# Heads of 64 columns: products that stream 128 columns and keep 64, in a kernel of three transformer blocks

## The chip, the cores and the metric

One core of a Trainium2 chip. The metric is the device time of one execution of the whole kernel, in microseconds; the time of a kernel is the median over its runs.

## What is computed

Three blocks over a sequence of 512 tokens of width 1024, in float32. Block 1 mixes with forgetting attention (4 heads), RWKV-7 (8 heads) and MoBA attention (4 heads); block 2 with gated linear attention and sparse attention chosen by an indexer (DSA, 8 heads on shared keys and values), then a gated unit and feed-forward parts; block 3 with a bidirectional state-space scan (32 heads in 8 groups) beside a convolution. Every head is 64 wide. What matters here, cut from the reference:

```python
# attention of blocks 1 and 2 (per head, d = 64)
probs = softmax(logits); y = einsum('bhqk,bhkd->bhqd', probs, v)
# RWKV-7, per head and token
removed = einsum('bhvk,bhk->bhv', state, kk_t)
state = state * w_t - removed (kk_t * a_t)^T + v_t k_t^T
y_t = einsum('bhvk,bhk->bhv', state, r_t)
y = ((y - mean) * rsqrt(var + GN_EPS)) * ln_w + ln_b      # over the 64 of a head
# scan, one direction, chunks of 128
mix = scores[..., None] * decay * dt
y_diag = einsum('bclsgr,bcsgrp->bclgrp', mix, xs)          # p = 64
y_off = einsum('bclgn,bcgrpn->bclgrp', cm, h_prev) * exp(la)
```

## The kernel before, in words

Activations lie as feature x token tiles of 128 x 512 or token x feature tiles of 128 x 512, four blocks of 128 tokens side by side. Two heads of 64 make a pair of 128, so a tile of tokens holds a pair's two heads side by side in each block of 128 columns. A projection weight is loaded by SP, split by ScalarE and VectorE into a high and a low part, and each of its products is three matmuls (L296 to L298, L370 to L372). The products named below are plain fp32.

- **Attention** (`attn`, L550 to L606; block 1 twice through `causal_attn`, block 2 through DSA). For each pair, query block and head: logits, softmax, transposes of the probabilities, and the product with the values (L583), which sums over the key blocks into `[:, :64]` of a PSUM tile; the evacuation scales the 64 columns into `yt` (L588 in block 1). The step before the value product is emitted one head ahead.
- **RWKV** (`rwkv_chain`, L803 to L906), one chain for each of four pairs, chunks of 128 tokens: decayed keys against values (`pv`, L841, copied by ScalarE, L842), the chain over chunks with `pU` (L855, read negated by ScalarE, L856) and the state, then the output `pY`: for each chunk the state's product (L877, both heads in 128 columns) and for each head the two products of the chunk itself (L879, L880; 64 columns each). Mean and variance over each head's 64 columns follow on VectorE, with ScalarE's square and POOL's power between (L885 to L894), then transposes (L898), the affine step, the bonus rows loaded by SP (L901), and the gate (L905). Each chain has two PSUM buffers under its tag.
- **Scan** (`ssm_group`, L1451 to L1534), 8 groups of 4 heads by 4 chunks: decays by ScalarE, added by POOL, multiplied with the scores by VectorE into `E` (L1504), four products with 64 columns each (`pY`, L1507), the state's product (`pO`, L1510), and VectorE's sums (L1518 and after). L1531 transposes the result.
- **Modulation sums** (`mod_tile`, L383 load, L384 row sum on VectorE) are spread over the stages; in block 1 they stand beside the RWKV tail.

What sets the order: strings of letters (`ORDER`, `REST`, `ORDER2`, `ORDER3`) say which generator emits its next step, and a scheduler then orders the instructions of all engines with its own costs for each; so a product of other shape moves its neighbours too. Each engine works its own queue in order; SP's queue holds the loads.

Of the kernel before, what the change touches and what calls it, by code (L numbers as in the profile page):

```python
# [12 lines left out]
OP = mybir.AluOpType  # L13
# [182 lines left out]
class Kern:  # L196
# [357 lines left out]
    def attn(self, npr, logits, value, ys, put, tag2="pt"):  # L554
# [16 lines left out]
        def second(pr, qt, hh, P, rinv):  # L571
# [9 lines left out]
            o = self.pst(tag2)[:, :64]  # L581
            for kb in range(qt + 1):
                nc.tensor.matmul(o, PT[:, kb * 128:(kb + 1) * 128], value(pr, hh, kb), start=kb == 0, stop=kb == qt)  # L583
# [26 lines left out]
    def causal_attn(self, q, k, v, ys, FHL=None):  # L610
# [16 lines left out]
        return self.attn(2, logits, lambda pr, hh, kb: v[kb][:, (2 * pr + hh) * 64:(2 * pr + hh) * 64 + 64], ys, put)  # L627
# [174 lines left out]
    def rwkv_chain(self, i, K, gl, out, tag):  # L802
# [35 lines left out]
        pv = ps()  # L838
        for hh in range(2):
            for m in range(4):  # L840
                nc.tensor.matmul(pv[:, hs(m, hh)], Ak[hh][:, MS[m]], tok["v"][:, hs(m, hh)], start=True, stop=True)  # L841
        nc.scalar.copy(RV, pv)  # L842
# [4 lines left out]
        nU = vM  # L847
        for n, ms in enumerate(MS):
# [5 lines left out]
            for hh in range(2):  # L854
                nc.tensor.matmul(pU[:, 64 * hh:64 * hh + 64], TF[hh][:, ms], RV[:, hs(n, hh)], start=True, stop=True)  # L855
            nc.scalar.mul(nU[:, ms], pU[:, 0:128], -1.0)  # L856
# [17 lines left out]
        pY = ps()  # L874
        for m, ms in enumerate(MS):
            if m:
                nc.tensor.matmul(pY[:, ms], RO[:, ms], S[:, ms], start=True, stop=False)  # L877
            for hh in range(2):
                nc.tensor.matmul(pY[:, hs(m, hh)], A[hh][0][:, ms], tok["v"][:, hs(m, hh)], start=m == 0, stop=False)  # L879
                nc.tensor.matmul(pY[:, hs(m, hh)], A[hh][1][:, ms], nU[:, hs(m, hh)], start=False, stop=m == 0 or hh == 1)  # L880
# [4 lines left out]
        nc.vector.tensor_reduce(sm, mh(pY), AX.X, OP.add)  # L885
        nc.vector.tensor_scalar(sm, sm, 1.0 / 64, None, OP.mult)
        b8 = lambda t: t.rearrange("p (a o) -> p a o", o=1).to_broadcast([128, 8, 64])
        nc.vector.tensor_tensor(y8, mh(pY), b8(sm), OP.subtract)
# [563 lines left out]
    def ssm_group(self, g, xs, dtv, pre=()):  # L1452
# [38 lines left out]
        for c in range(4):  # L1491
# [14 lines left out]
            for r in range(4):  # L1506
                nc.tensor.matmul(pY[:, r * 64:(r + 1) * 64], M[:, r * 128:(r + 1) * 128], XT[c][:, r * 64:(r + 1) * 64], start=True, stop=True)  # L1507
# [10 lines left out]
            nc.vector.tensor_tensor(y, pY[:, :256], sk, OP.add)  # L1518
# [258 lines left out]
    def dsa(self, bq, bk2, bv, masks, ys):  # L1777
# [9 lines left out]
        return self.attn(4, logits, lambda pr, hh, kb: bv[:, kb], ys, lambda p: self.split(p, "scalar", "vector", tag="g"), "pb")  # L1787
# [127 lines left out]
    def block2_attn(self):  # L1915
# [21 lines left out]
        bv = self.small([128, 4, 64], "bv", bufs=1)  # L1937
# [6 lines left out]
        nc.scalar.copy(bv, pt[:, :, 0:64])  # L1944
# [186 lines left out]
```

## Time and profile before

| what | value |
|---|---|
| median of 3 runs | 3138.52 us (3137.82 to 3141.42) |
| the profiled execution | 3126.9 us |
| its span | 3125.1 us |
| mean granted clock of TensorE | 0.977 |
| TensorE busy | 2941.1 us (94%) |
| VectorE busy | 2044.3 us (65%) |
| ScalarE busy | 1158.7 us (37%) |
| GpSimd busy | 663.6 us (21%) |

Busy time is a union over an engine's instructions; the profile's two shares of TensorE (PE for matmuls, PEld for weight loads) overlap. Lines are those of the kernel before. The granted clock is the share of full speed that TensorE was given in a stretch. A fp32 matmul leaves two records and two weight loads.

### The profile page before, as it was taken

The numbers are of one execution on the slowest core, as the hardware profiler recorded it, in microseconds if no ns is written. First come the engines' busy times: TensorE is split into PE (matmuls) and PEld (weight loads), VectorE is DVE, ScalarE is ACT, GpSimd is POOL, SyncE is SP. The second block draws the span as 40 slices with busy tenths as digits, with TensorE's granted clock in tenths as the row PEclk, the third lists the DMA queues.
The fourth block names the chain that finished last, engine by engine and source line by source line (L and its number), as shares of the span: only waits on it lengthen the run. The fifth ranks groups of instructions, "written<-read, shape, count | busy, mean of one in ns | idle before, by whom it ended". The sixth has DMA issues, their size and how long they took to land. (4 is left out here: it accounts for less than half of the span.)

```text
span 3125.1 us, 39947 instructions
## 1 busy us (share of the span) xinstructions
PE 2941.1 (94%) x15254; PEld 2428.6 (78%) x15254; DVE 2044.3 (65%) x3398; ACT 1158.7 (37%) x1927; POOL 663.6 (21%) x574
## 2 busy tenths in 40 slices
PE   5999999999989979999999999999899999989998
PEld 3778778888867778888889788887777777777877
DVE  7766477666467677566655565464888989886254
ACT  4433433323333544332334243233433333434232
POOL 3222011000234253200011110002223343441011
PEclk9998999999999999999999999999999999999999
DMA  6334034363312133236343222332222122212342
GB/s 223 102 106 144 11 112 157 110 207 95 99 58 88 44 99 98 88 93 204 100 152 101 88 82 90 106 91 79 85 71 66 63 78 71 71 58 88 115 128 81
DMA packets 137376, 312.53 MB, mean 100 GB/s; under 512 B 25504, under 2 KB 51680, under 8 KB 137184
## 3 DMA queue, kind: packets, MB, share of 16 engines
q1 hardware_dynamic: 137184, 309.98, 32.0%
q8 instruction: 120, 1.97, 0.3%
q14 instruction: 72, 0.59, 0.1%
HBM read 296.82 MB, written 13.11 MB: 99 GB/s over the span
## 5 line engine op out<-in xcount | busy, mean ns | idle before, releaser
L275 ACT CAST wh<-wr 128x1024 fp32r<-128x1024 f32 (+2 forms) x457 | 455.6, 997 | 1010.7 <-PE mm L297 517.8
L277 DVE TENSOR_TENSOR wl<-wr,wh 128x1024 fp32r<-128x1024 f32 (+2 forms) x415 | 499.3, 1203 | 503.6 <-ACT wh L275 496.0
L298 PE MATMUL mm<-hi,wl 128*128 128x512 f32 (+1 forms) x1780 | 683.4, 384 | 10.4 <-DVE wl L277 10.3
L296 PE MATMUL mm<-hi,wh 128*128 128x512 f32 (+1 forms) x1780 | 685.7, 386 | 4.5 <-DVE cv L1217 2.6
L297 PE MATMUL mm<-lo,wh 128*128 128x512 f32 (+1 forms) x1780 | 684.3, 385 | 1.3 <-POOL lo L494 0.6
L298 PEld LDWEIGHTS mm<-hi,wl 128*128 128x128 f32 x1780 | 339.3, 191 | 77.9 <-DVE wl L277 12.8
L296 PEld LDWEIGHTS mm<-hi,wh 128*128 128x128 f32 x1780 | 339.0, 191 | 74.5 <-issue 3.7
L297 PEld LDWEIGHTS mm<-lo,wh 128*128 128x128 f32 x1780 | 339.5, 191 | 68.7 <-issue 2.2
L286 POOL CAST hi<-us 128x512 fp32r<-128x512 f32 x66 | 42.4, 643 | 872.8 <-DVE us L1194 855.1
L298 PE MATMUL pt<-hi,wl 128*128 128x512 f32 (+1 forms) x517 | 188.5, 365 | 4.0 <-DVE wl L277 4.0
L296 PE MATMUL pt<-hi,wh 128*128 128x512 f32 (+1 forms) x517 | 188.1, 364 | 0.0
L297 PE MATMUL pt<-lo,wh 128*128 128x512 f32 (+1 forms) x517 | 187.6, 363 | 0.0
L296 PE MATMUL pb<-hi,wh 128*128 128x512 f32 (+1 forms) x477 | 178.2, 374 | 0.0
L297 PE MATMUL pb<-lo,wh 128*128 128x512 f32 (+1 forms) x477 | 177.9, 373 | 0.0
L298 PE MATMUL pb<-hi,wl 128*128 128x512 f32 (+1 forms) x477 | 177.8, 373 | 0.0
L1415 DVE SCALAR_TENSOR_TENSOR u<-csg,vec,u 128x400 f32<-128x400 f32 (+7 forms) x208 | 165.2, 796 | 2.5
L298 PE MATMUL pa<-hi,wl 128*128 128x512 f32 (+1 forms) x420 | 160.9, 383 | 0.0
L296 PE MATMUL pa<-hi,wh 128*128 128x512 f32 (+1 forms) x420 | 160.6, 382 | 0.0
L297 PE MATMUL pa<-lo,wh 128*128 128x512 f32 (+1 forms) x420 | 160.6, 382 | 0.0
L370 PE MATMUL mm<-wh,hi 128*128 128x256 f32 (+1 forms) x512 | 150.6, 295 | 9.4 <-DVE sar L1984 3.0
L371 PE MATMUL mm<-wl,hi 128*128 128x256 f32 (+1 forms) x512 | 147.7, 289 | 0.5 <-DVE wl L277 0.5
L372 PE MATMUL mm<-wh,lo 128*128 128x256 f32 (+1 forms) x512 | 147.7, 289 | 0.3 <-DVE lo L494 0.3
(758 smaller groups left out, 5589.7 us busy)
## 6 DMA issues: line engine op xcount, KB each, us to landing
wr<-f_up SPq DMA_DIRECT2D x88, 512.0 KB, 3.5
wm<-w_mod SPq DMA_DIRECT2D x152, 256.0 KB, 5.1
wr<-w3x SPq DMA_DIRECT2D x56, 512.0 KB, 3.5
wr<-w_up SPq DMA_DIRECT2D x44, 512.0 KB, 3.6
wr<-w3c SPq DMA_DIRECT2D x40, 512.0 KB, 3.6
wr<-f_down SPq DMA_DIRECT2D x32, 512.0 KB, 3.5
wr<-w SPq DMA_DIRECT2D x29, 512.0 KB, 3.7
wr<-w_down SPq DMA_DIRECT2D x16, 512.0 KB, 3.6
```

The source lines that it names most:

```text
L275: nc.scalar.copy(h, r)
L277: self.lo_engs[self.nlo % len(self.lo_engs)].tensor_tensor(l, r, h.bitcast(FT), OP.subtract)
L286: getattr(nc, hi_eng).tensor_copy(h, x)
L296: nc.tensor.matmul(ps, a, xh, start=first and i == 0, stop=False)
L297: nc.tensor.matmul(ps, a, xl, start=False, stop=False)
L298: nc.tensor.matmul(ps, b, xh, start=False, stop=last and i == n - 1)
L370: nc.tensor.matmul(ps, xh, a, start=k == 0, stop=False)
L371: nc.tensor.matmul(ps, xh, b, start=False, stop=False)
L372: nc.tensor.matmul(ps, xl, a, start=False, stop=k == K - 1)
L1415: nc.vector.scalar_tensor_tensor(r8(o)[:, :, a:b], src, w(k), r8(o)[:, :, a:b], OP.mult, OP.add)
```

## The change

Each product with 64 moving columns streams both heads of a pair (in DSA, with its shared values, the next key block too, with a fifth block of zeros at the end) into twice the PSUM columns, and the reader of the product takes the 64 columns that count. In RWKV `pv` and `pY` become one PSUM tile for each head; the state's product is then made for both of them, and the reads of `pY` are split into two ops each.

```diff
--- before.py
+++ after.py
@@ -578,9 +578,12 @@
                 nc.scalar.copy(PT, psP)
             else:
                 nc.vector.tensor_copy(PT, psP)
-            o = self.pst(tag2)[:, :64]
+
+            o = self.pst(tag2)[:, :128]
             for kb in range(qt + 1):
-                nc.tensor.matmul(o, PT[:, kb * 128:(kb + 1) * 128], value(pr, hh, kb), start=kb == 0, stop=kb == qt)
+                v, at = value(pr, hh, kb)
+                nc.tensor.matmul(o, PT[:, kb * 128:(kb + 1) * 128], v, start=kb == 0, stop=kb == qt)
+            o = o[:, at:at + 64]
             if pr not in yts:
                 yts[pr] = self.small([128, 512], "yt", bufs=1)
             yo = yts[pr][:, qt * 128 + hh * 64:qt * 128 + hh * 64 + 64]
@@ -624,7 +627,7 @@
                 nc.tensor.matmul(ps, self.selR[:, h * 128:(h + 1) * 128], FHL[:, :nk], start=False, stop=False)
             nc.tensor.matmul(ps[:, qt * 128:nk], self.identR, self.mnegR, start=False, stop=True)
 
-        return self.attn(2, logits, lambda pr, hh, kb: v[kb][:, (2 * pr + hh) * 64:(2 * pr + hh) * 64 + 64], ys, put)
+        return self.attn(2, logits, lambda pr, hh, kb: (v[kb][:, pr * 128:pr * 128 + 128], 64 * hh), ys, put)
 
 
     def mix_evac(self, ps, j, out):
@@ -835,11 +838,13 @@
 
         RV = self.t2(nm="RV", tag="i")
         Ak = inner(kt, KA, 1)
-        pv = ps()
+
+        of = lambda t, hh: t.rearrange("p (m h d) -> p m h d", m=4, h=2)[:, :, hh]
         for hh in range(2):
-            for m in range(4):
-                nc.tensor.matmul(pv[:, hs(m, hh)], Ak[hh][:, MS[m]], tok["v"][:, hs(m, hh)], start=True, stop=True)
-        nc.scalar.copy(RV, pv)
+            pv = ps()
+            for ms in MS:
+                nc.tensor.matmul(pv[:, ms], Ak[hh][:, ms], tok["v"][:, ms], start=True, stop=True)
+            nc.scalar.copy(of(RV, hh), of(pv, hh))
         yield
 
         S = self.t2(nm="S", tag="h")
@@ -852,8 +857,8 @@
                 nc.vector.tensor_tensor(RV[:, ms], pK[:, 0:128], RV[:, ms], OP.add)
             pU = ps()
             for hh in range(2):
-                nc.tensor.matmul(pU[:, 64 * hh:64 * hh + 64], TF[hh][:, ms], RV[:, hs(n, hh)], start=True, stop=True)
-            nc.scalar.mul(nU[:, ms], pU[:, 0:128], -1.0)
+                nc.tensor.matmul(pU[:, 128 * hh:128 * hh + 128], TF[hh][:, ms], RV[:, ms], start=True, stop=True)
+            nc.scalar.mul(nU[:, ms].rearrange("p (h d) -> p h d", h=2), pU[:, 0:256].rearrange("p (b d) -> p b d", b=4)[:, 0:4:3], -1.0)
             if n < 3:
                 pS = ps()
                 nc.tensor.matmul(pS[:, 0:128], tok["k"][:, ms], tok["v"][:, ms], start=True, stop=False)
@@ -871,21 +876,24 @@
             yield
         A = list(zip(inner(kt, RO, 0), inner(bt, RO, 0, d2, "g")))
         yield
-        pY = ps()
+        pYs = [ps(), ps()]
         for m, ms in enumerate(MS):
-            if m:
-                nc.tensor.matmul(pY[:, ms], RO[:, ms], S[:, ms], start=True, stop=False)
-            for hh in range(2):
-                nc.tensor.matmul(pY[:, hs(m, hh)], A[hh][0][:, ms], tok["v"][:, hs(m, hh)], start=m == 0, stop=False)
-                nc.tensor.matmul(pY[:, hs(m, hh)], A[hh][1][:, ms], nU[:, hs(m, hh)], start=False, stop=m == 0 or hh == 1)
+            for hh, pY in enumerate(pYs):
+                if m:
+                    nc.tensor.matmul(pY[:, ms], RO[:, ms], S[:, ms], start=True, stop=False)
+                nc.tensor.matmul(pY[:, ms], A[hh][0][:, ms], tok["v"][:, ms], start=m == 0, stop=False)
+                nc.tensor.matmul(pY[:, ms], A[hh][1][:, ms], nU[:, ms], start=False, stop=True)
         yt = self.t2(nm="yt")
 
         sm = self.small([128, 8], "gns")
         y8 = mh(yt)
-        nc.vector.tensor_reduce(sm, mh(pY), AX.X, OP.add)
+        sh = sm.rearrange("p (m h) -> p m h", h=2)
+        for hh, pY in enumerate(pYs):
+            nc.vector.tensor_reduce(sh[:, :, hh], of(pY, hh), AX.X, OP.add)
         nc.vector.tensor_scalar(sm, sm, 1.0 / 64, None, OP.mult)
         b8 = lambda t: t.rearrange("p (a o) -> p a o", o=1).to_broadcast([128, 8, 64])
-        nc.vector.tensor_tensor(y8, mh(pY), b8(sm), OP.subtract)
+        for hh, pY in enumerate(pYs):
+            nc.vector.tensor_tensor(of(yt, hh), of(pY, hh), sh[:, :, hh:hh + 1].to_broadcast([128, 4, 64]), OP.subtract)
         nc.scalar.activation(out, yt, AF.Square)
         va = self.small([128, 8], "gnv")
         nc.vector.tensor_reduce(va, out.rearrange("p (a d) -> p a d", d=64), AX.X, OP.add)
@@ -1504,7 +1512,8 @@
             nc.vector.tensor_tensor(v4(M), v4(E[0]), b4(SC[:, cs]), OP.mult)
             pY = self.pst("pt")
             for r in range(4):
-                nc.tensor.matmul(pY[:, r * 64:(r + 1) * 64], M[:, r * 128:(r + 1) * 128], XT[c][:, r * 64:(r + 1) * 64], start=True, stop=True)
+                nc.tensor.matmul(pY[:, r * 128:(r + 1) * 128], M[:, r * 128:(r + 1) * 128], XT[c][:, r // 2 * 128:r // 2 * 128 + 128], start=True, stop=True)
+            pY = pY.rearrange("p (a b q) -> p a b q", a=2, b=4)[:, :, 0:4:3]
             pO = self.pst("pt")
             for d, k in ((0, c), (1, 3 - c)):
                 nc.tensor.matmul(pO[:, d * 256:(d + 1) * 256], Cf[:, cs], H[k][:, d * 256:(d + 1) * 256], start=True, stop=True)
@@ -1515,7 +1524,8 @@
             sk = self.t2(nm="sk", tag="t")[:, :256]
             nc.gpsimd.tensor_tensor(q4(sk), q4(XT[c]), self.dsk[:, 4 * g:4 * g + 4].rearrange("p (h o) -> p h o", o=1).to_broadcast([128, 4, 64]), OP.mult)
             nc.gpsimd.tensor_tensor(T[:, :256], T[:, :256], T[:, 256:], OP.add)
-            nc.vector.tensor_tensor(y, pY[:, :256], sk, OP.add)
+            h4 = lambda t: t.rearrange("p (a b q) -> p a b q", a=2, b=2)
+            nc.vector.tensor_tensor(h4(y), pY, h4(sk), OP.add)
             nc.vector.tensor_tensor(y, y, T[:, :256], OP.add)
             nc.vector.scalar_tensor_tensor(y, y, 0.5, SZ[c // 2][:, (c % 2) * 256:(c % 2 + 1) * 256], OP.mult, OP.mult)
             nc.scalar.activation(sk, y, AF.Square, accum_out=ss[:, c:c + 1])
@@ -1784,7 +1794,7 @@
             nc.tensor.matmul(ps, q[:, qt * 128:nk], bk2[1][:, :nk], start=False, stop=False)
             nc.tensor.matmul(ps, self.identR, self.mnegR if qt == 0 else masks[qt], start=False, stop=True)
 
-        return self.attn(4, logits, lambda pr, hh, kb: bv[:, kb], ys, lambda p: self.split(p, "scalar", "vector", tag="g"), "pb")
+        return self.attn(4, logits, lambda pr, hh, kb: (bv[:, kb:kb + 2], 0), ys, lambda p: self.split(p, "scalar", "vector", tag="g"), "pb")
 
     def gla_decay(self, alr):
 
@@ -1934,14 +1944,15 @@
             nc.scalar.copy(bk2[0][e:e + 64], kk[64:128])
         for e in (0, 64):
             nc.vector.tensor_tensor(bk2[1][e:e + 64], kk[64:128], bk2[0][64:128].bitcast(FT), OP.subtract)
-        bv = self.small([128, 4, 64], "bv", bufs=1)
+        bv = self.small([128, 5, 64], "bv", bufs=1)
+        nc.gpsimd.memset(bv[:, 4], 0.0)
         iw = self.small([128, 4, 4], "iw", bufs=1)
         alr = self.t2(nm="alr")
         nc.gpsimd.memset(alr[0:64], 0.0)
         nc.gpsimd.memset(alr[32:33], 1.0)
         t, pt = self.fm_tok(A["w2s"], 100, xs)
         nc.scalar.copy(alr[0:16], t[64:80])
-        nc.scalar.copy(bv, pt[:, :, 0:64])
+        nc.scalar.copy(bv[:, 0:4], pt[:, :, 0:64])
         nc.scalar.mul(iw, pt[:, :, 96:100], 0.5 * 0.125)
         masks = {}
         idx = self.indexer(iq, ik2, iw, masks)
```

The built order of each engine changes in the three stages that hold these lines. Three places:

TensorE, the output products of RWKV's first chain (`pa` is the chain's PSUM tile, `tokv` the values, `x` the tile that holds U, `S` the state, `RO` the decayed receptance, `pt` attention's), as before:

```order
L879 MATMUL pa_3654<-tokv_2817,Ak_3556 128x64
L880 MATMUL pa_3654<-x_70,Ak_3570 128x64
L879 MATMUL pa_3654<-tokv_2817,Ak_3558 128x64
L880 MATMUL pa_3654<-x_70,Ak_3575 128x64
L877 MATMUL pa_3654<-S_3115,RO_456 128x128
L879 MATMUL pa_3654<-tokv_2817,Ak_3556 128x64
L880 MATMUL pa_3654<-x_70,Ak_3570 128x64
L879 MATMUL pa_3654<-tokv_2817,Ak_3558 128x64
L880 MATMUL pa_3654<-x_70,Ak_3575 128x64
L877 MATMUL pa_3654<-S_3115,RO_456 128x128
```

and now (L883 is before's L877, L884 and L885 are L879 and L880, L696 a product of another chain's blocks):

```order
L884 MATMUL pa_3662<-tokv_2817,Ak_3564 128x128
L885 MATMUL pa_3662<-x_70,Ak_3578 128x128
L883 MATMUL pa_3662<-S_3123,RO_456 128x128
L884 MATMUL pa_3663<-tokv_2817,Ak_3566 128x128
L885 MATMUL pa_3663<-x_70,Ak_3583 128x128
L884 MATMUL pa_3662<-tokv_2817,Ak_3564 128x128
L696 MATMUL mm_3602<-RO_1216,bt_1235 128x128 x3
L696 MATMUL mm_3603<-RO_1216,bt_1235 128x128 x3
L696 MATMUL mm_3602<-RO_1216,bt_1235 128x128
L696 MATMUL mm_3603<-RO_1216,bt_1235 128x128
L885 MATMUL pa_3662<-x_70,Ak_3578 128x128
```

Two PSUM tiles are filled side by side, all with 128 columns; products of other chains stand between.

VectorE, the tail of RWKV, from chain 2's first reduce (`mm_3716`) to chain 3's subtraction, as before (`wm` is a row of the modulation weights, L384; `gns` and `gnv` are sum and variance):

```order
L885 TENSOR_REDUCE gns_3737<-mm_3716 128x8
L384 SCALAR_TENSOR_TENSOR wm_4014,rawo<-wm_4014,act 128x512
L891 TENSOR_REDUCE gnv_3711<-x_75 128x8
L886 TENSOR_SCALAR gns_3737<-gns_3737 128x8
L885 TENSOR_REDUCE gns_3768<-mm_3747 128x8
L892 TENSOR_SCALAR gnv_3711<-gnv_3711 128x8
L888 TENSOR_TENSOR yt_3736<-mm_3716,gns_3737 128x512
L894 TENSOR_TENSOR yt_3705<-yt_3705,gnv_3711 128x512
L886 TENSOR_SCALAR gns_3768<-gns_3768 128x8
L563 TENSOR_REDUCE nmx_3781<-pt_3778 128x1
L891 TENSOR_REDUCE gnv_3742<-x_76 128x8
L888 TENSOR_TENSOR yt_3767<-mm_3747,gns_3768 128x512
```

and now, from chain 2's variance to chain 3's first reduce (`mm_3773`; L892, L899, L900 and L902 are before's L885, L891, L892 and L894):

```order
L384 SCALAR_TENSOR_TENSOR wm_4104,rawo<-wm_4104,act 128x512
L568 RECIPROCAL rinv_3818<-sm_3816 128x1
L384 SCALAR_TENSOR_TENSOR wm_4108,modr<-wm_4108,act 128x512
L899 TENSOR_REDUCE gnv_3768<-x_76 128x8
L1152 TENSOR_TENSOR modr<-modr,rawo 128x1
L384 SCALAR_TENSOR_TENSOR wm_4111,rawo<-wm_4111,act 128x512
L900 TENSOR_SCALAR gnv_3768<-gnv_3768 128x8
L384 SCALAR_TENSOR_TENSOR wm_4152,modr<-wm_4152,act 128x512
L902 TENSOR_TENSOR yt_3760<-yt_3760,gnv_3768 128x512
L1152 TENSOR_TENSOR modr<-modr,rawo 128x1
L384 SCALAR_TENSOR_TENSOR wm_4155,rawo<-wm_4155,act 128x512
L892 TENSOR_REDUCE gns_3798<-mm_3773 128x4
```

Between chain 0's first reduce and chain 3's variance stand 17 rows of L384 now, 6 before, and chain 2's normalisation is finished ahead of chain 3's first reduce.

TensorE, the scan, second group, second chunk (`mm` is the projection beside it, `hi` and `lo` its activations, `wh` and `wl` its weights; `E` the masked decays), as before:

```order
L298 MATMUL mm_19786<-hi_18155,wl_19789 128x512
L296 MATMUL mm_19786<-hi_18157,wh_19788 128x512
L297 MATMUL mm_19786<-lo_18158,wh_19788 128x512
L298 MATMUL mm_19786<-hi_18157,wl_19789 128x512
L1507 MATMUL pt_19768<-tok_19463,E_19764 128x64 x4
L1510 MATMUL pt_19773<-H_19499,sfm_19276 128x256
L1510 MATMUL pt_19773<-H_19505,sfm_19276 128x256
L296 MATMUL mm_19786<-hi_18159,wh_19788 128x512
```

and now (numbers of these tiles are 33 higher; L1515 is before's L1507, L1519 is L1510):

```order
L297 MATMUL mm_19819<-lo_18187,wh_19821 128x512
L298 MATMUL mm_19819<-hi_18186,wl_19822 128x512
L296 MATMUL mm_19819<-hi_18188,wh_19821 128x512
L1515 MATMUL pt_19801<-tok_19496,E_19797 128x128 x4
L1519 MATMUL pt_19806<-H_19532,sfm_19309 128x256
L1519 MATMUL pt_19806<-H_19538,sfm_19309 128x256
L297 MATMUL mm_19819<-lo_18189,wh_19821 128x512
L298 MATMUL mm_19819<-hi_18188,wl_19822 128x512
```

Before, the four products follow the last matmul with `hi_18157`; now they follow the first with the tile that was `hi_18155` (18188 - 33): five matmuls earlier.

## Rows read from the trace of the kernel before

**Rows 1.** The page, part 1: busy time, share of the span and instructions of TensorE.

```profile
PE 2941.1 (94%) x15254; PEld 2428.6 (78%) x15254; DVE 2044.3 (65%) x3398; ACT 1158.7 (37%) x1927; POOL 663.6 (21%) x574
```

**Rows 2.** Windows: stretch, busy of PE, PEld, DVE, ACT, POOL, granted clock, DMA.

```profile
313.00:437.00 124.00, 121.61 (x890) 97.61 (x889) 62.09 (x181) 48.31 (x143) 9.87 (x12) 1.00 0.15 50
405.00:428.00 23.00, 23.00 (x212) 21.65 (x210) 16.50 (x50) 4.19 (x12) 2.01 (x1) 1.00 0.41 137
437.00:450.00 13.00, 8.93 (x37) 6.91 (x38) 8.73 (x17) 4.67 (x10) 6.01 (x5) 0.74 0.07 21
450.00:480.00 30.00, 30.00 (x132) 24.16 (x131) 25.41 (x57) 11.83 (x17) 5.94 (x4) 1.00 0.51 158
1090.00:1250.00 160.00, 135.97 (x928) 123.13 (x927) 119.53 (x215) 71.89 (x142) 67.09 (x42) 0.95 0.32 99
2270.00:2840.00 570.00, 531.54 (x2709) 428.13 (x2708) 501.43 (x704) 214.25 (x371) 212.20 (x194) 0.97 0.22 70
```

**Rows 3.** Timeline of TensorE, 420.5 to 422.2 us: start, length, line, operands, records merged.

```profile
420.66 0.44 PE L877 MATMUL mm<-S,RO 128*128 128x128 f32 x2
...
421.55 0.39 PE L880 MATMUL mm<-x,Ak 128*128 128x64 f32 x2
421.77 0.44 PE L877 MATMUL mm<-S,RO 128*128 128x128 f32 x2
```

**Rows 4.** Timeline of TensorE at 2373 and 2482 us: eight records each.

```profile
2372.97 1.10 PE L1507 MATMUL pt<-tok,E 128*128 128x64 f32 x8
2481.90 1.06 PE L1472 MATMUL pa<-sfm,sfm 128*128 128x128 f32 x8
```

**Rows 5.** Chain of waits, 2268 to 2278 us: start, length, what.

```profile
2273.03 0.84 PE pt L1507 x8
2273.87 0.92 PE pt L1510 x4
```

**Rows 6.** Lines L1507 and L1472: durations in ns, least, median, most.

```profile
L1507 PEld LDWEIGHTS pt<-tok,E x256: 186/192/338, 2272.8 to 2821.7; 128*128 128x128 f32 x128
L1507 PE MATMUL pt<-tok,E x256: 218/275/422, 2272.9 to 2821.7; 128*128 128x64 f32 x128
L1472 PE MATMUL pa<-sfm,sfm x64: 275/275/348, 2259.0 to 2764.8; 128*128 128x128 f32 x64
```

**Rows 7.** Timeline of VectorE, 413 to 438 us; brackets: idle before, and releaser.

```profile
413.21 0.69 DVE L885 TENSOR_REDUCE gns<-pa 128x8 f32<-128x512 f32 x1 [0.94 <-PE pa L880]
416.54 0.56 DVE L563 TENSOR_REDUCE nmx<-pt 128x1 f32<-128x384 f32 x1 [1.16 <-PE pt L625]
419.30 0.69 DVE L885 TENSOR_REDUCE gns<-pb 128x8 f32<-128x512 f32 x1 [0.92 <-PE pb L880]
422.95 0.68 DVE L384 SCALAR_TENSOR_TENSOR wm<-wm,act 128x512 f32<-128x512 f32 x1
428.45 0.69 DVE L885 TENSOR_REDUCE gns<-mm 128x8 f32<-128x512 f32 x1 [2.27 <-PE mm L880]
437.53 0.67 DVE L891 TENSOR_REDUCE gnv<-x 128x8 f32<-128x512 f32 x1
```

**Rows 8.** Groups by line and shape, whole span, VectorE and ScalarE: busy, mean ns.

```profile
L563 DVE TENSOR_REDUCE nmx<-pt 128x1 f32<-128x256 f32 x16 | 6.8, 422 | 6.9 <-PE pt L625 5.7 <-PE pt L1785 1.0
L1518 DVE TENSOR_TENSOR Y<-pt,sk 128x256 f32<-128x256 f32 x32 | 13.3, 415 | 0.0
L842 ACT COPY RV<-mm 128x512 f32<-128x512 f32 x2 | 1.2, 586 | 0.9 <-PE mm L841 0.9
L578 ACT COPY PT<-pt 128x256 f32<-128x256 f32 x8 | 2.9, 364 | 0.0
```

**Rows 9.** Waits of TensorE, 2270 to 2840 us: total, times, longest.

```profile
PE pa L1531 <- DVE Y L1527: 13.9, 12, 2.6
PE pt L1507 <- DVE E L1504: 12.4, 14, 2.6
```

## The prediction

> **What bounds the kernel now.** I read the page's busy times first, then the windows of the stages that the change touches, then single lines. TensorE is busy 94% of the span [rows 1]: what TensorE issues and what it waits for sets the time, and the other engines count only where TensorE waits for them. The change touches three stages: the mixing stage of block 1 up to 450 us (attention and RWKV), sparse attention in block 2 (1020 to 1250 us) and the scan of block 3 (2270 to 2840 us). In the windows [rows 2] see that TensorE is full from 405 to 428 us and from 450 to 480 us, that between them lies a tail (437 to 450 us) with 8.93 of 13 us busy and a granted clock of 0.74, and that in the scan VectorE is close behind TensorE, 501 of 570 us against 532.
>
> **Part 1: 64 columns become 128.** Each fp32 matmul is two records. From the loops: 320 records in attention values (80 matmuls each in block 1 and block 2), 256 in RWKV (128 matmuls), 256 in the scan [rows 6], 832 in all. What does a record with 64 columns hold TensorE for, from start to start? Between the two starts of L877 [rows 3] lie ten records, two with 128 columns and eight with 64, in 421.77 - 420.66 = 1.11 us: 111 ns each. The wide kind alone: eight records of L1472 take 1.06 us from first start to last end, the last being 0.275 long [rows 4, 6], so (1.06 - 0.275) / 7 = 112 ns. Eight of L1507, with 64 columns, give (1.10 - 0.275) / 7 = 118 by the same count and 0.84 / 8 = 105 in the chain of waits [rows 4, 5]. The median duration is 275 ns for both widths [rows 6]. So I put the price of the added columns at **0**. What fills the slot instead is the weight load in front of each record, 128 columns and 192 ns long for either kind [rows 6], overlapping its neighbours. Bounds: below, nothing, since no row has a wide record faster; above, the slope from 128 to 256 columns, (230 - 112) / 128 = 0.92 ns a column (L1510's 0.92 / 4 [rows 5]), which is a rival below.
>
> The Trainium skill, page "TensorE: Matmul & The Clock Gate", section "Back-to-back issue gap", speaks against this change: it gives an isolated matmul of up to 64 columns about 60 cycles and one of 128 columns 134, so the columns would cost, and nearly double. The rows disagree, as 105 to 118 and 112 ns stand side by side. The same page's section on LDWEIGHTS lets a load's time go by its own columns, 128 / 1.2 = 107 ns as an estimate, whatever is streamed after it, and with that the 111 ns agree.
>
> **Part 2: RWKV output products.** With a tile for each head the state product (L877, 12 matmuls over four chains) is done for both heads: 12 more matmuls, 24 records. At 0.111 us, in a stretch (405 to 428 us) where TensorE has no gap [rows 2], this is **+2.7 us**. Bounds: 0 if they fall into the tail's idle time, 5.3 if at half clock.
>
> **Part 3: halved evacuations.** L885 and L888 (0.69 us) become two ops of half the columns; the nearest row is the 256-column reduce, 0.422 us [rows 7, 8], so each costs 2 x 0.422 - 0.69 = 0.15 more, eight times 1.2 us on VectorE. Half of it, the later two chains, has no other work in front of it: **+0.6 us** (bounds 0 and 1.2). The value copy L842 (0.586) becomes two, 2 x 0.364 [rows 8]: 0.14 x 4 = 0.6 us on ScalarE, 48 of 124 us busy [rows 2], at 0; without that cover 0.6.
>
> **Part 4: the tail of RWKV.** This is the order's doing. Between chain 0's first reduce (L885, 413.21 us) and chain 3's second (L891, 437.53 us) [rows 7] VectorE's queue holds 6 row sums of the modulation (L384); in the changed order 17 stand there. Eleven more at 0.68 [rows 7] are 7.5 us on the path of the normalisation, which must end before the output projection gets its RWKV rows. What can swallow them is the time in which VectorE waited for TensorE there: 0.94, counted at the start of the stretch and so left out, then 1.16 + 0.92 + 2.27 = 4.4 us [rows 7]. The waits for POOL's power stay, since as before at most one such sum stands between. I take 7.5 - 4.4 = **+3.1 us**, with 0 and 7.5 as bounds. It is lost for good, as TensorE is full right after, 30 of 30 us [rows 2]. The four loads of the bonus rows (L901) move behind eight more modulation loads on SP's queue, but as before the load ahead of them waits for a tile that chain 3's last products read, so they leave at the same event: 0.
>
> **Part 5: the scan.** The four output products of a chunk wait for VectorE's mask product E (L1504): 12.4 us, 14 times [rows 9]. In the changed order about 21 of 32 groups stand earlier among the wide projection matmuls, mostly by two to twelve of them. Where VectorE sets the pace, an earlier place only moves the wait and lets the projection fill the time behind it, so one group's shift is paid, not each: five matmuls of 0.23 (nearest row: L1510's record [rows 5]), **+1.1 us**. Bounds 0 and 18, the sum of the shifts of the groups at which TensorE waits already. The strided read of the products (L1518, 0.415 us [rows 8]) has the same elements: 0; if it ran like a 512-element read (0.69), 32 x 0.275 = 8.8 us more on VectorE, which has 69 us free [rows 2].
>
> **Part 6: the rest.** The memset of the padding block is POOL work early in a stretch where POOL is busy 67 of 160 us [rows 2]: 0. The strided read of the chain's U (L856) is the same 128 elements: 0. Sparse attention is re-ordered widely, with as many groups earlier as later and TensorE idle 24 of 160 us [rows 2]: 0, within 5 us either way.
>
> **Sum:** 0 + 2.7 + 0.6 + 3.1 + 1.1 = +7.5 us. The durations are from an execution of 3126.9 us, 11.6 us under the median of the runs shown; on it the sum gives 3134.4, on the median **3146.0 us**. A measurement can tell about 0.2%, 6.3 us, from no change: slower is over 3144.8, faster under 3132.2.
>
> **The rivals.** (B) *Columns set the price.* At 0.92 ns, 64 x 832 columns are 49 us, with the rest 3195 us. Against it stand ten records in 1.11 us. The page's rule above would do just this. Chance 0.03. (C) *The scan pays each earlier place.* If VectorE falls back with TensorE, each wait is new: 18 us in place of 1.1, 3163 us. For it speaks that VectorE is 88% busy there; against, that the wait at one group gives slack at the next. It decides once L1507's wait for E is over some 20 us in place of 12.4. Chance 0.17. (D) *The other side: the new order frees the scan.* The transposes L1531 wait 13.9 us for Y and the products 12.4 for E [rows 9]; outputs made earlier let Y be done earlier. If half of the 26.3 us go, -13.1 + 6.4 from parts 2 to 4 gives 3131.8; it decides once more than 6.4 us of these waits vanish. Chance 0.20. (E) *The clock.* Twice the columns keep the array busier; the stretches below full clock lose 13 x 0.26 + 160 x 0.05 + 570 x 0.03 = 28.5 us [rows 2]. A third back, with the rest, is 3136.5 us. Against it: in 313 to 437 us, where the RWKV products with 64 columns lie, the clock is 1.00 already [rows 2], and the low stretch of the tail is one of waits. Chance 0.10. That the change doesn't do what it says is out: the built order has 128 columns at every such line.
>
> **The numbers.** The forecast has 0.50, between 3138.5 and 3153. Faster: three quarters of D, a little of E, and a tenth of the forecast's own case, in which the order gains some us: 0.24. Same: 0.22 of the forecast's case, where part 2 or 4 is hidden, and most of E: 0.31. Slower: the rest of the forecast's case, C and B: 0.45. The range goes down to 3124, D with 20 of the 26 us gone and part 4 hidden, and up to 3164, C.
>
> **What would show it.** Part 1: L585, L1515 and L884 at 110 to 118 ns from start to start, as L1472 before; over 130 is B. Part 2: 48 records of L883, TensorE still full there. Part 4: chain 3's L899 some 3 to 6 us later than 437.5, little wait on TensorE ahead of L892. Part 5: L1515's wait for E between 11 and 16 us. E shows in the granted clock of 437 to 450 and of the scan. The prediction is wrong if the three stages together move less than 3 us, or if a stage untouched moves.

## The result and the profile after

The changed kernel takes 3173.5 us (median of four runs, 3165.05 to 3181.69), the kernel before 3138.17 in the runs beside it: a ratio of 1.0118 [1.0093, 1.0143]. That is slower, by 37 us by the ratio (35 between the medians), where 7.5 were forecast, and above the range, which ended at 3164. The profiled execution took 3165.05 us, its span is 3163.2.

The page's busy times, as in [rows 1]; 24 more records on TensorE, eight more ops on VectorE:

```profile
PE 2957.9 (94%) x15278; PEld 2440.2 (77%) x15278; DVE 2034.8 (64%) x3406; ACT 1157.0 (37%) x1931; POOL 658.5 (21%) x575
```

To find where the time went I took TensorE's first or last record of lines that both kernels have as marks, and compared the stretches between them. Two stretches grew: the mixing of block 1 (from the first L621 to the first L461) and the scan (from the first L1564 to the last L410). The others, sparse attention among them, stand within 3 us. Windows of the kernel before over these two, columns as in [rows 2], and over its first stage, for the last section:

```profile
0.00:295.00 295.00, 245.49 (x1254) 194.18 (x1254) 201.04 (x430) 107.47 (x168) 86.18 (x78) 0.94 0.45 141
295.00:489.00 194.00, 185.03 (x1210) 150.48 (x1209) 115.08 (x286) 77.11 (x196) 29.97 (x28) 0.96 0.26 82
2241.00:2842.00 601.00, 558.49 (x2850) 447.70 (x2850) 528.70 (x738) 227.38 (x393) 225.56 (x205) 0.97 0.22 69
```

The same stretches of the changed kernel, and the two windows that answer to the tail and the scan of [rows 2]:

```profile
293.00:497.00 204.00, 191.66 (x1235) 156.18 (x1235) 113.18 (x294) 76.71 (x200) 29.65 (x28) 0.97 0.24 79
2252.00:2881.00 629.00, 565.63 (x2850) 451.10 (x2849) 522.45 (x738) 227.40 (x392) 219.34 (x205) 0.96 0.21 66
...
430.00:459.00 29.00, 21.35 (x117) 16.44 (x117) 23.12 (x64) 11.54 (x23) 11.06 (x7) 0.88 0.40 135
2279.00:2879.00 600.00, 540.62 (x2715) 433.45 (x2716) 497.15 (x706) 215.41 (x373) 205.98 (x194) 0.96 0.21 66
```

See that the mixing is 10 us longer and the scan 28, and that in the scan the same 2850 records are issued: TensorE's idle time there is 629 - 565.63 = 63.4 us, against 601 - 558.49 = 42.5 before. That is 21 of the 28 us; the other 7 are busy time, the same records at a granted clock of 0.96 in place of 0.97. VectorE is idle longer too, 106.6 us against 72.3. Neither engine has more to do; both wait more. One such window is good to a few us: four other kernels below whose scan has no edit took 601 to 607 us over it.

TensorE's waits in the scan, as in [rows 9] (L1515 is the old L1507, L1541 the old L1531):

```profile
PE pt L1515 <- DVE E L1512: 20.0, 19, 2.5
PE pa L1541 <- DVE Y L1537: 17.8, 9, 4.6
PE mm L296 <- DVE cv L1225: 6.6, 4, 4.2
PE pa L1437 <- POOL acc L1429: 3.6, 1, 3.6
```

The wait for E is 20.0 us in place of 12.4, that for Y 17.8 in place of 13.9. For E, 11 to 16 us were forecast.

TensorE at the widened RWKV products (L884 and L885, the old L879 and L880), as in [rows 3]:

```profile
418.77 0.39 PE L884 MATMUL pb<-tokv,Ak 128*128 128x128 f32 x2
418.99 0.39 PE L885 MATMUL pb<-x,Ak 128*128 128x128 f32 x2
419.21 0.39 PE L884 MATMUL pb<-tokv,Ak 128*128 128x128 f32 x2
...
434.89 0.52 PE L906 MATMUL pb<-cst,yt 128*128 128x128 f32 x3 [3.17 <-DVE gns L893]
435.89 0.46 PE L884 MATMUL mm<-tokv,Ak 128*128 128x128 f32 x2 [0.49 <-DVE yt L896]
```

Pairs of 128-column records start 0.22 us apart, 110 ns each: the columns cost nothing here. The last two lines belong to the tail: chain 3's products begin at 435.89 us, with TensorE idle for 3.17 and 0.49 us just before, where in the kernel before they followed chain 2's in a full stretch [rows 2]. On VectorE, as in [rows 7], the first reduce (L892, the old L885), the last row sum of the normalisation (L899, the old L891) and the last gate product (L913) stand at:

```profile
418.30 0.42 DVE L892 TENSOR_REDUCE gns<-pa 128x4 f32<-128x256 f32 x1 [1.73 <-PE pa L885]
...
446.65 0.69 DVE L899 TENSOR_REDUCE gnv<-x 128x8 f32<-128x512 f32 x1 [0.22 <-ACT x L897]
...
457.92 0.69 DVE L913 TENSOR_TENSOR x<-x,mm 128x512 f32<-128x512 f32 x1 [1.39 <-POOL x L910]
```

The last row sum is 9.1 us later than the 437.53 of before; 3 to 6 were forecast. But 5.1 of these 9.1 us stand already at the first reduce, 418.30 against 413.21 [rows 7]. From the first reduce to the last row sum it is 28.4 us against 24.3, 4.0 more. The last gate product comes 39.6 us behind the first reduce here, and 34.7 in the kernel before, where it stands at:

```profile
447.94 0.69 DVE L905 TENSOR_TENSOR x<-x,mm 128x512 f32<-128x512 f32 x1 [3.03 <-PE mm L904]
```

### The profile page after: what moved, and what is told of

Read it like the earlier page. It is cut to its first block, busy times and chain, and to the rows that moved or that the text cites. A ratio compares the mean times of both kernels' runs of the same rounds, so it can differ in the third digit from the quotient of the medians.

```text
span 3163.2 us, 39996 instructions
## 1 busy us (share of the span) xinstructions
PE 2957.9 (94%) x15278; PEld 2440.2 (77%) x15278; DVE 2034.8 (64%) x3406; ACT 1157.0 (37%) x1931; POOL 658.5 (21%) x575
## 5 line engine op out<-in xcount | busy, mean ns | idle before, releaser
L1423 DVE SCALAR_TENSOR_TENSOR u<-csg,vec,u 128x432 f32<-128x432 f32 (+8 forms) x208 | 159.2, 766 | 2.6
```

The lines of the kernel that those rows point to most:

```text
L1423: nc.vector.scalar_tensor_tensor(r8(o)[:, :, a:b], src, w(k), r8(o)[:, :, a:b], OP.mult, OP.add)
```

## The experiments

Two questions: do the columns cost anything, and if not, which piece of the new order costs 28 us in the scan and 10 us in block 1? A list of order-only dependencies between neighbours on each engine holds an order; kernels marked "pinned" carry it:

```diff
+PIN = {
...
+}
+def pin(tc, nc):
+    dep = mybir.DependencyInfo(mybir.DependencyClass.NoSync, mybir.DependencyReason.DATA)
...
+                tc.add_manual_dep(ins[at], prev.name, dep)
...
+        pin(tc, tc.nc)
```

**How small differences are read.** Runs of one kernel differ in their mean granted clock: in the twenty runs of the kernel before that stand beside scan_products_early, spans went from 3118.8 us at 0.977 to 3164.5 at 0.962. Span times clock stayed between 3043 and 3050 in all twenty. This product, the "clocked span" below, scatters from run to run with a standard deviation of 2 to 4 us (the clock is given to 0.001, which is 3 us), and its mean over the kernel before was 3046 to 3048 in every group of runs, so its mean shows differences of a few us. It leaves out what a lower clock costs, so the ratio stands beside it, and a loss by the ratio can be two or three times the loss by clocked span. The changed kernel's is 3080.4, 33 us more.

### Columns or order

**cols_order_kept**: 640 of the 832 records get 128 columns (both attentions, `pU`, the scan), in the order of the kernel before (pinned).

```diff
-                nc.tensor.matmul(pY[:, r * 64:(r + 1) * 64], M[:, r * 128:(r + 1) * 128], XT[c][:, r * 64:(r + 1) * 64], start=True, stop=True)
+                nc.tensor.matmul(pY[:, r * 128:(r + 1) * 128], M[:, r * 128:(r + 1) * 128], XT[c][:, r // 2 * 128:r // 2 * 128 + 128], start=True, stop=True)
...
+        pin(tc, tc.nc)
```

> 640 of the 832 records stream 128 columns (attention values of both blocks, pU of RWKV, the scan's products); pv and pY of RWKV stay as before; every engine's instructions are held in the order of the kernel before. Theory ORDER (the loss is the new order's, the columns are free): no change, 3138 us within 6, the scan 2270 to 2840 us as long as before within 3 us, 111 to 118 ns a record. Theory COLUMNS (the 64 further columns cost time in the array, in PSUM or in the clock): 640/832 of the 35 us, about +27 us, 3165 us, spread over the three stages by their records, and over 130 ns a record or a lower granted clock.

Measured: 3143.18 us against 3146.16, ratio 1.000 [0.9975, 1.0025], clocked span +2. Its scan, by marks, stands within 3 us of the 601 of before, at the same clock:

```profile
2249.00:2853.00 604.00, 558.90 (x2853) 448.88 (x2854) 528.92 (x739) 228.21 (x394) 225.19 (x205) 0.97 0.21 69
```

Within that interval the columns of these 640 records are free; for all 832 rival B had made 49 us of them. The other 192, RWKV's `pv` and `pY`, were not held in the old order; their price is read from the 110 ns of `pY` above.

**scan_free**: only the scan's products get 128 columns, and the scheduler orders freely. The diff is the one above without the pin.

> Only the scan's products stream 128 columns; the scheduler orders freely. ORDER: the +28 us that the scan lost in the changed kernel, 3160 to 3168 us, all of it between 2270 and 2840 us. COLUMNS: 256/832 of 35 us, +11 us, 3149 us.

Measured: 3163.05 us, 1.009 [1.0056, 1.0124], clocked span +18.

**scan_64_new_order**: the kernel before, 64 columns everywhere, pinned to the order of scan_free. The diff is the pin alone.

> The kernel before, 64 columns everywhere, with every engine's instructions held in the order that the scheduler chose for scan_free. ORDER: as slow as scan_free within 4 us, +28 us. COLUMNS: as the kernel before, 3138 us.

Measured: 3175.04 us, 1.0108 [1.0077, 1.014], clocked span +17. Without a single added column the order alone brings the loss of scan_free. Windows of its first stage (for the last section) and of its scan by marks:

```profile
0.00:305.00 305.00, 256.44 (x1255) 204.08 (x1255) 201.77 (x432) 107.52 (x168) 87.14 (x78) 0.90 0.44 137
...
2252.00:2889.00 637.00, 575.99 (x2847) 459.48 (x2847) 522.74 (x738) 228.31 (x394) 218.51 (x205) 0.94 0.21 65
```

In the scan 61 us are idle, 18.5 more than before, and a clock of 0.94 in place of 0.97: busy time grows by 17.5 us for the same records. A lower clock goes with the slow orders: this kernel and the three slow ones below (64 columns all) ran the scan at 0.94, scan_free and the changed kernel at 0.96, and the kernel before, cols_order_kept and the four kernels whose scan has no edit at 0.97. It does not follow the waits alone, as scan_state_first, with fewer of them, stood at 0.96. With this order the scan had 0.96 in scan_free with 128 columns and 0.94 here with 64, one profile each; whether the width holds the clock up there stays open.

### Which piece of the scan's order

**scan_first_group_new** and **scan_later_groups_new**: 64 columns, pinned to the new order in the first of the scan's eight groups only, or in all but the first. In the first, the new order puts one state product (L1510) 97 rows behind its partner; the theory DISPLACED says that this one step costs the time. The diffs are pins alone.

> 64 columns everywhere; every engine in scan_free's order up to the last state product of the scan's first group, and in the order of the kernel before from there. Theory DISPLACED (one matmul, the second half of the first chunk's state product L1510, stands 97 rows later in the new order, with it the sums L1513 and L1518 stand behind weight splits on VectorE, and the next chunk's E comes late): 7 to 11 us over the kernel before. Theory EARLIER PLACES (each group's products stand earlier and each pays the wait for E): 4 of 32 groups, +3.5 us.

> The complement: the order of the kernel before through the scan's first group, scan_free's order after it, 64 columns. DISPLACED: the +28 us of scan_free less 7 to 11, +17 to +21 us. EARLIER PLACES: 28 of 32 groups, +24.5 us.

Measured: 1.0015 [0.9982, 1.0049], +3 clocked, and 1.0109 [1.0076, 1.0143], +13. DISPLACED falls, as the first group was to cost 7 to 11 us by it; the loss lies in the later groups. By the ratio these lose 34 us, by clocked span 13; EARLIER PLACES had 24.5.

**scan_products_early** (pinned, 64 columns): only TensorE's order changes. In the kernel as built nineteen groups of output products (the expectation counts twenty) go ahead of 2 to 11 other matmuls, 88 in all, as in the new order. The theory EARLIER PLACES says that each such place is paid; its rival, FILLERS, that VectorE's order is to blame. One of the groups, rows of TensorE's order:

```
 L296 MATMUL mm_19786<-hi_18155,wh_19788 128x512
+L1507 MATMUL pt_19768<-tok_19463,E_19764 128x64 x4
+L1510 MATMUL pt_19773<-H_19499,sfm_19276 128x256
+L1510 MATMUL pt_19773<-H_19505,sfm_19276 128x256
 L297 MATMUL mm_19786<-lo_18156,wh_19788 128x512
...
 L298 MATMUL mm_19786<-hi_18157,wl_19789 128x512
-L1507 MATMUL pt_19768<-tok_19463,E_19764 128x64 x4
```

> 64 columns, the order of the kernel before on every engine but TensorE, where 20 of the scan's product groups (four L1507, two L1510; chunks 4 to 27) are moved ahead of as many projection matmuls as in scan_free's order (2 to 11). Theory EARLIER PLACES (TensorE stands at E with the projection's matmuls behind it): most of the loss of scan_later_groups_new, +10 to +20 us in time and TensorE's wait for E 8 us or more over the 12.4 of before. Theory FILLERS (VectorE's convolution taps L1415 were moved ahead of the scan's own sums): no change, within 4 us.

Measured: 3175.67 us, 1.0135 [1.0094, 1.0177], clocked span +13. By the ratio that is 42 us, over the 10 to 20 expected, as its runs had a mean clock of 0.963 against 0.971. Its scan (window by marks), and the waits of all engines in that window:

```profile
2264.00:2899.00 635.00, 579.12 (x2851) 461.76 (x2850) 527.74 (x737) 226.51 (x393) 224.50 (x205) 0.94 0.21 65
```

```profile
ACT wh L275 <- PE mm L297: 157.3, 40, 11.8
...
PE pt L1507 <- DVE E L1504: 27.6, 21, 3.6
...
DVE T L1513 <- PE pt L1510: 13.9, 14, 2.1
...
PE pa L1531 <- DVE Y L1527: 11.2, 10, 2.1
```

The first and the third of these waits in the scan of the kernel before (2241 to 2842 us):

```profile
ACT wh L275 <- PE mm L297: 101.5, 34, 7.4
...
DVE T L1513 <- PE pt L1510: 9.5, 13, 3.4
```

TensorE's wait for E grows by 15.2 us, the wait for Y gives back 2.7. At 0.23 us a matmul [rows 5] the 88 places are 20 us, so the earlier places are paid for the most part, not once.

**scan_taps_early** (pinned, 64 columns): only VectorE's order changes. The convolution taps (L1415) stand ahead of the scan's own ops, as in the new order (FILLERS). Rows of VectorE's order at one place:

```
 L1395 SCALAR_TENSOR_TENSOR csg_19095<-csg_19095,mm_19033 128x512
+L1412 TENSOR_SCALAR u_19444<-csg_19095,vec_18363 128x8x49
+L1415 SCALAR_TENSOR_TENSOR u_19444<-csg_19095,vec_18363,u_19444 128x8x50
+L1415 SCALAR_TENSOR_TENSOR u_19444<-csg_19095,vec_18363,u_19444 128x8x51
+L1415 SCALAR_TENSOR_TENSOR u_19444<-csg_19095,vec_18363,u_19444 128x8x52
 L1513 TENSOR_TENSOR T_19156<-pt_19153,EL_18640 128x512
```

> The counterpart: 64 columns, the order of the kernel before on every engine but VectorE, where the convolution taps (L1415, with L1411 and L1412) stand ahead of the same instruction of the scan as in scan_free's order; the scan's own instructions keep their order. FILLERS: +10 to +20 us, E and the sums L1513 to L1520 late. EARLIER PLACES: no change, within 4 us.

Measured: 3169.26 us, 1.0116 [1.0077, 1.0156], clocked span +12.5. Window by marks and waits:

```profile
2258.00:2893.00 635.00, 576.11 (x2852) 458.54 (x2852) 530.74 (x738) 227.93 (x392) 219.76 (x205) 0.94 0.21 65
```

```profile
PE pt L1507 <- DVE E L1504: 19.5, 17, 2.5
PE pa L1531 <- DVE Y L1527: 13.7, 11, 2.9
```

So each of the two moves alone, TensorE's or VectorE's, brings by clocked span what scan_later_groups_new loses (13), and the whole order brings 17: the two do not add up. Each theory had put the other's move at no change, and both moves cost. My reading, which no run isolates, is that both take away the distance between E's making and its use. In scan_taps_early the wait for E grows by 7.1 us only, while TensorE's idle time in the scan grows by 16.4 (58.9 against 42.5).

### The other way round

**scan_state_first**: 64 columns, in the order of before (pinned), but in all 32 chunks the state's products, which need no E, are issued ahead of the four that do. In this kernel L1510 is the masked product.

```diff
-            pY = self.pst("pt")
-            for r in range(4):
...
             pO = self.pst("pt")
...
+            pY = self.pst("pt")
+            for r in range(4):
...
```

> 64 columns, the order of the kernel before on every engine but for one exchange in each of the scan's 32 chunks: TensorE does the state product (two matmuls of L1510, 0.92 us) ahead of the four products that wait for E. If TensorE's waits for E set the scan's pace, the state product fills up to 0.9 us of each of the 14 waits: 5 to 10 us faster, 3128 to 3133 us, and L1513 starts earlier. If VectorE's own queue sets it, no change, 3138 us within 4.

Measured: 3129.44 us, 0.9976 [0.9947, 1.0005], clocked span -9. TensorE's wait for E falls to 6.4 us:

```profile
PE pt L1510 <- DVE E L1504: 6.4, 9, 1.7
```

**scan_products_late** and **scan_products_later**: beside that, in nine chunks the products stand one to eight projection matmuls later, and in the second kernel more of them, at seven further waits.

> scan_state_first with one more edit: in the nine chunks in which TensorE still waits for E there, the four products stand one to eight projection matmuls later (as many as fill the wait). If the place of the products sets the wait: TensorE's wait for E falls from 6.4 to under 2 us and the time by another 3 to 5 us, to some 3122 to 3127 us, faster than the kernel before by 10 to 13. If the wait only moves to Y (L1531, 14.0 us): as scan_state_first.

> scan_products_late with the seven waits for E that remain (3.5 us) filled in the same way, the products two to four projection matmuls later. If the places set the waits: another 1 to 3 us, some 10 to 14 us under the kernel before. If VectorE's own queue now sets the pace: as scan_products_late, 11 us under.

Measured: 3124.25 us, 0.9977 [0.9945, 1.0009], -11 clocked; and 3126.1 us, 0.9942 [0.9909, 0.9975], -10. The first set of moves brought 2 us and left a wait for E of 3.5 us, where under 2 was expected. The two kernels stand level in clocked span, so the second set brought nothing. Waits and the window of the later one:

```profile
PE pa L1531 <- DVE Y L1527: 13.7, 12, 2.9
PE pa L1297 <- DVE xw L1291: 4.4, 4, 3.0
PE pt L1510 <- DVE E L1504: 3.6, 3, 1.9
```

```profile
2257.00:2846.00 589.00, 554.48 (x2847) 446.70 (x2846) 527.83 (x738) 226.56 (x392) 225.97 (x205) 0.98 0.23 70
```

The wait for E is nearly gone, 3.6 us in place of 12.4, the scan takes 589 us in place of 601, and the clock there is 0.98. This order, with 64 columns, is 0.6% faster than the kernel before by its ratio (0.3% by clocked span; the ratio of scan_products_late, with the same clocked span, does not exclude no change) and some 1.8% faster than the changed one (1.0118 / 0.9942). The wait for Y did not move.

### Block 1 and attention

**rwkv_free**: only the RWKV part of the change, ordered freely.

```diff
-        pY = ps()
+        pYs = [ps(), ps()]
...
-        nc.vector.tensor_reduce(sm, mh(pY), AX.X, OP.add)
+        for hh, pY in enumerate(pYs):
+            nc.vector.tensor_reduce(sh[:, :, hh], of(pY, hh), AX.X, OP.add)
```

> Only RWKV's products are changed (two tiles for pv and pY, 24 more records, halved reads); the scheduler orders freely. ORDER: the +10 us that block 1 lost in the changed kernel, 3146 to 3150 us, the scan as before. COLUMNS: 256/832 of 35 us for the columns and 2.7 for the records, +13 us, 3151 us; the two differ here only in whether the records' spacing grows.

Measured: 3146.38 us, 1.002 [0.999, 1.005], clocked span +4.5. Its first reduce, last row sum and last gate product on VectorE, with 17 modulation sums between the first two:

```profile
424.47 0.42 DVE L889 TENSOR_REDUCE gns<-pa 128x4 f32<-128x256 f32 x1 [0.40 <-PE pa L882]
...
452.07 0.67 DVE L896 TENSOR_REDUCE gnv<-x 128x8 f32<-128x512 f32 x1
...
463.51 0.69 DVE L910 TENSOR_TENSOR x<-x,mm 128x512 f32<-128x512 f32 x1 [1.18 <-POOL x L907]
```

From the first reduce it is 27.6 us to the last row sum and 39.0 to the last gate product.

**rwkv_other_tag**: the same, but the fourth chain's two output tiles come from another PSUM tag, so that its products need not wait for chain 2's buffers. TWO BUFFERS says that this wait, the 3.17 us above among it, makes the late tail.

```diff
-        pYs = [ps(), ps()]
+        pYs = [self.pst("pa" if i == 3 else tag) for _ in range(2)]
```

> rwkv_free with one more edit: the two output tiles of the fourth chain come from the PSUM tag of the first chain, not from the tag that it shares with the third. Theory TWO BUFFERS (the tag has two buffers and each chain now takes both, so the fourth chain's products wait for the third's subtractions, 7.5 us in the changed kernel's trace): block 1 gives back 5 to 8 us, total 3138 to 3143 us, and the fourth chain's products follow the third's at once. Theory QUEUED SUMS (the eleven more modulation sums on VectorE make the tail late): as rwkv_free, 3146 us.

Measured: 3146.51 us, 1.0035 [1.0009, 1.0061], +6.6. The fourth chain's products followed at once, and no time was gained. The same three places:

```profile
419.66 0.42 DVE L889 TENSOR_REDUCE gns<-pa 128x4 f32<-128x256 f32 x1 [0.40 <-PE pa L882]
...
443.54 0.68 DVE L896 TENSOR_REDUCE gnv<-x 128x8 f32<-128x512 f32 x1
...
456.72 0.68 DVE L910 TENSOR_TENSOR x<-x,mm 128x512 f32<-128x512 f32 x1
```

The last row sum comes 23.9 us after the first reduce, as before the change, but the last gate product 37.1. The wait for buffers does make the row sum late; that it costs the kernel 5 to 8 us, as TWO BUFFERS has it, is not borne out.

**rwkv_sums_late**: rwkv_free's order (pinned), but the modulation sums behind the sixth stand after the last gate product, and the bonus loads eight places earlier on SP's queue. QUEUED SUMS is my part 4.

> rwkv_free with its own order held, but on VectorE the modulation sums (L384) after the sixth behind the first chain's reduce stand behind the last gate product of the four chains, and on SP the four loads of the bonus rows stand eight loads earlier, as in the kernel before. Theory QUEUED SUMS (they make the tail of RWKV late): 3 to 5 us faster than rwkv_free, the last gate product within 4 us of the kernel before. Theory SERIAL CHAINS (the fourth chain's products still wait for the third's subtractions, since both share two buffers): the tail stays long, no more than 2 us faster.

Measured: 3151.87 us, 1.003 [0.9998, 1.0062], +7.5. It is no faster than rwkv_free, but that does not refute QUEUED SUMS, as its trace shows: the same three places, with 6 sums between the first two, and one of TensorE:

```profile
425.28 0.42 DVE L889 TENSOR_REDUCE gns<-pa 128x4 f32<-128x256 f32 x1 [0.40 <-PE pa L882]
...
450.23 0.69 DVE L896 TENSOR_REDUCE gnv<-x 128x8 f32<-128x512 f32 x1 [1.48 <-ACT x L894]
...
460.65 0.69 DVE L910 TENSOR_TENSOR x<-x,mm 128x512 f32<-128x512 f32 x1 [2.17 <-POOL x L907]
```

```profile
471.42 0.79 PE L297 MATMUL mm<-lo,wh 128*128 128x512 f32 x1 [8.34 <-DVE lo L287]
```

From the first reduce it is 25.0 us to the last row sum and 35.4 to the last gate product, within 1 us of the kernel before. But behind the gate product fourteen sums now stand ahead of the split (L287) that the output projection needs, and TensorE waits 8.34 us for it. So the sums do lengthen the tail, and what they cost the kernel is not settled by this run.

**attention_free**: only the attention part (320 records, both blocks), ordered freely.

```diff
-                nc.tensor.matmul(o, PT[:, kb * 128:(kb + 1) * 128], value(pr, hh, kb), start=kb == 0, stop=kb == qt)
+                v, at = value(pr, hh, kb)
+                nc.tensor.matmul(o, PT[:, kb * 128:(kb + 1) * 128], v, start=kb == 0, stop=kb == qt)
```

> Only the attention values stream 128 columns (320 records, both blocks, with the padding block and its memset); the scheduler orders freely. By the sum of the other parts (scan_free and rwkv_free together leave some 5 to 10 us of the changed kernel's loss) ORDER says +3 to +10 us, 3142 to 3148; COLUMNS, with nothing for 640 records in cols_order_kept, has no loss left to give: no change.

Measured: 3151.04 us, 1.0042 [1.0017, 1.0067], clocked span +6.6. The same records cost nothing in cols_order_kept, so this too is order. In its one profile the mixing of block 1 took 206 us at 0.92 against 194 at 0.96, which is 3 more in length times clock; the rest of the loss could not be placed.

The three parts alone add up to 18 + 4.5 + 6.6 = 29 of the 33 us of the whole change.

## Why the prediction was wrong

- **Part 1, columns at 0: right.** 110 ns from start to start, and 640 doubled records at 1.000 [0.9975, 1.0025]. The issue gaps that the page "TensorE: Matmul & The Clock Gate" of the Trainium skill gives for an isolated matmul, by which they would have cost, do not carry over to this stream of fp32 products, each behind a weight load of 128 columns; here the measurement decides.
- **Parts 2 to 4, +6.4 us in RWKV: size about right, cause shown in part.** RWKV alone gave +4.5 clocked, 6 us by its ratio with an interval from -3 to +16. Part 4 put 3.1 us between the first reduce and the last row sum; the changed kernel has 4.0 there, and in rwkv_free, with 17 sums, it is 2.7 us longer than in rwkv_sums_late, with 6. The wait for PSUM buffers, which part 4 did not name, is in it too: without it these 27.6 us are 23.9. The other 5.1 of the 9.1 us arise ahead of the first reduce, where the prediction had at most part 2's 2.7; why stays open. These are single profiles. What was not tried: both edits at once with the sums behind the splits, each pair of tiles side by side in one PSUM tile, and another order of the four chains.
- **Part 5, the scan at +1.1: the step that failed.** The term measured +28 us in the profiles (629 against 601), and +17 clocked for the order alone, over its upper bound of 18 in the first and close to it in the second. The false sentence was "an earlier place only moves the wait and lets the projection fill the time behind it, so one group's shift is paid, not each". In scan_products_early nineteen earlier places cost 15.2 us in waits for E and got 2.7 back at Y. That the loss is not given back is measured; why is my reading. A late TensorE is not caught up by VectorE, as VectorE's next inputs come from the same TensorE: there VectorE waits longer for the state's product (13.9 us against 9.5), and ScalarE waits longer to split the next weights (157.3 us against 101.5). No run isolates these two waits, and in scan_taps_early only the first of them grows (18.5 us; ScalarE's stays at 102.1).
- **What part 5 left out.** I compared only TensorE's order around the products. VectorE's order had moved as well, its taps ahead of the scan's own ops, and that alone costs 1.0116 [1.0077, 1.0156]. And the clock was left out: beside 18.5 us more idle time, scan_64_new_order ran its scan at 0.94 in place of 0.97.
- **Part 6:** sparse attention is level, as forecast; the attention part as a whole, put at 0, cost +6.6 clocked.
- **The rivals.** C was the mechanism as far as TensorE's order goes, at 0.17 and priced at 18 us; its turning point, a wait for E of some 20 us, was just reached at 20.0. By clocked span the scan cost what C says, 17 to 18, but in part by luck: C counted TensorE's shifts alone and not VectorE's moves, and the 28 of the profiles holds a lower clock that it did not count. B fell with part 1. D did not come with this change, but exists: made on purpose, scan_products_later has it in part, 10 us clocked where D had 13. E did not come, as the scan's clock went down, not up; with the order held it stayed at 0.97.

## What to carry to other kernels

When a scheduler orders the program, a change of shape is two changes. Pin the old order to price the shape, and pin the new order on the old shape to price the order; here the first was 0 and the second 17 of the 18 us. In a loop of two engines that feed each other, compare the order of both, and count an in-order wait moved ahead of its filler as paid at each place, for the most part (13 of 20 us here). Where a product waits for another engine, issue first what does not need that input (here -9 us by clocked span).

## What was not expected of the hardware

The scatter between runs of one kernel is that of the granted clock: in the twenty runs named above, spans from 3118.8 to 3164.5 us came with clocks from 0.977 to 0.962, and the product stayed between 3043 and 3050. In the profiles it sits mostly in the first 500 us. The first stage took 295 us at 0.94 in the profile of the kernel before and 305 at 0.90 in that of scan_64_new_order (the first rows of their windows above), which has the same instructions there and no edit. The mixing of block 1 took 194 us at 0.96 in the kernel before and 201 at 0.93 in scan_products_later, which has no edit there either. Ten us of difference between two profiles can thus be the clock of one execution, before any edit has had its say.
